# Joining the products of V of an attention head, and planning the order of a kernel's work in ten stretches

## The chip, the core and the metric

The kernel runs on one core of one Trainium2 chip. The metric is the time of the whole program on the device, in microseconds (us), as the median of several runs. Engines carry two names here: TensorE is PE in the profile (PEld are its weight loads), VectorE is DVE, ScalarE is ACT, GpSimd is POOL, and SyncE, which issues the transfers, is SP.

## What is computed

The reference is a backbone of two layers over 512 latent tokens and 256 context tokens of width 1024, in float32. Layer 0 attends to a neighbourhood on a grid with a position bias, layer 1 to a sliding window with grouped keys, sink logits and rotary embedding; latent queries see their local keys and all context keys in one softmax.

```
for i in range(2):
    u = modulate(rms_norm(h, g_mix[i]), shift1, scale1)
    q, k, v = projections of u, normed per head        # 16 heads of 64
    p = softmax(q k^T / 8 (+ bias or mask or sink), over local and context keys)
    h = h + gate1 * ((p v) @ wo)
    h = h + gate2 * (relu(modulate(rms_norm(h, g_mlp[i]), shift2, scale2) @ w1) ** 2 @ w2)
```

Shifts, scales and gates come from `ada_w`, a matrix of 1024 x 6144 for each layer. In layer 0 the context tokens are also queries, over the context alone.

## The kernel before

**Products.** Weights and activations are each split in a high and a low part (type fp32r), and a product is the sum of three on TensorE with 128 columns of the array (`mm`, `scores`, `proj1`). Products of V and the probabilities are done otherwise. V of a head has 64 columns, so `mm_halves` (line 722) issues two products for two different blocks of keys, one on columns 0 to 63 and one on columns 64 to 127 of the array; both halves add up in one PSUM bank, and `merge` (line 1103) adds the upper half to the lower with one copy and one addition. These products are in plain float32, which TensorE does in two passes. Two passes of two products make four records in the trace, shown as `128*64`. The modulation of layer 0 (`ada_pe`, line 787) uses 32 columns at a time (`128*32`).

**A head of layer 0** (`attn0`, line 1111; two heads to each of eight pairs `p`): scores of four blocks of queries and of the context; exponentials; probabilities scaled; then blocks of 128 x 128 transposed on TensorE into one of three PSUM banks (2, 3, 6), each bank copied to one of five slots of SBUF (`PTr`, `evac_pt`), and four calls of `mm_halves`: context keys, two of local keys, then the context's own queries. Latent and context sums take turns in bank 7.

**A head of layer 1** (`Head1`, line 1777): the same in `front` (scores, mask, exponentials) and `back` (transpositions, copies to three slots of `PTr`, line 1621, and three calls of `mm_halves` into bank 7). The front of a head is woven with the back of the one before, and the projections of the next four heads (`q1`) go between. Where the last heads run, the output projection (`wo1`) begins. Residuals `h` wait in DRAM during layer 1 and come back through four slots of SBUF (`h_slots`, line 1868).

**The order of the work** is not that of the code. All calls are recorded as steps of a plan with the steps that they depend on (`Plan.add`), each with a cost on its engine (`cost`, line 218). On TensorE a change between kinds of product has a cost of its own (`TURN`, line 291: "R" for 128 columns, "t" for transpositions, 64 and 32). `forward` (line 326) plays the plan once: each engine takes the ready step of lowest rank, and some steps choose between engines. `hurry` moves steps forward on whose account TensorE stood idle, `shaken` changes ranks at random, and `search` (line 464) keeps the best of many plays. It does so in two stretches: up to a step in the middle of the MLP of layer 0, judged by the start of that step, and from there to the end. Then every step is issued at one line (542), which the framework keeps in program order on each engine, with waits where data or buffers demand them. So every row of the trace names line 542, and rows are told apart by engine, operation and shapes.

Of the kernel before, what the change touches and what calls it, by code (L numbers as in the profile page):

```python
# [118 lines left out]
class Plan:  # L119
# [98 lines left out]
    def cost(self, x):  # L218
        if x.eng == "PE":
            kinds = []  # L220
            for f, args, kw in x.calls:
                out, a, b = args[:3]
                if f == "transpose":
                    kinds.append(("t", 128, 0, 128))
                else:
                    st, mv = a, b
                    kinds.append(("r" if st.dtype == R32 else "f", width(st)[0], geometry(out)[1], width(mv)[0]))
            kind, cols, _, n = kinds[0]
            if kind == "t":
                x.mode, x.occ, x.dur = "t", 109.0, 272.0  # L230
            elif kind == "r":
                x.occ, x.dur = ((n + 32) / 2.4 if n > 128 else 90.0), 389 - (512 - n) / 2.4
            elif cols == 128:
                x.occ = 2 * (n / 1.2 + 6)
                x.dur = x.occ + 150
            else:
                x.mode = cols
                at, runs = 999, []
                for _, _, p0, m in kinds:
                    if p0 <= at:  # L240
                        runs.append(0)
                    at = p0
                    runs[-1] = max(runs[-1], m)
                x.occ = sum(2 * (m / 1.2 + (47 if cols == 64 else 3)) for m in runs)
                x.dur = x.occ + 150
        elif x.eng == "SP":
            out, src = x.writes[0], x.reads[0]
            n, run = width(out)[0] * geometry(out)[2], 4 * min(geometry(y)[4][-1][1] for y in (out, src))
            if self.space(out) == "DRAM":
                n = math.prod(c for _, c in out.ap)  # L250
            x.bytes = 4 * n / (360.0 if run >= 2048 else 330.0 if run >= 1024 else 200.0 if run >= 512 else 100.0)
            x.occ = 620.0 if self.space(out) == "DRAM" else 430.0
        else:
# [210 lines left out]
    def search(self, rounds, tries, cut):  # L464
# [7 lines left out]
        rnd = random.Random(1)  # L472

        def of(rank, first, upto):
            s = self.forward(rank, first.copy(), upto)
            s.rank, s.last = rank, s.start[cut] if upto else max(s.end)
            return s

        def rounds_of(rank, first, upto, n, least=200):
            best = None  # L480
            for k in range(n):
                s = of(rank, first, upto)
                if not best or s.last < best.last:
                    best = s
                rank = self.hurry(rank if s.last < best.last * 1.004 else best.rank, s, least)
            return best

        first, rank = self.begin(), [float(x.i) for x in self.steps]
        for upto in (cut, None):
            found = [rounds_of(rank, first, upto, 3 * rounds)]  # L490
            for k in range(tries):
                found.sort(key=lambda s: s.last)
                found.append(rounds_of(self.shaken(found[k % 2].rank, rnd), first, upto, rounds, rnd.choice((100, 200))))
            first = best = min(found, key=lambda s: s.last)
        s = best
        for i, e in enumerate(s.eng):
            x = self.steps[i]
            if x.forms:
                x.eng = self.ALL[e]
                x.calls = [x.forms[x.eng]]  # L500
        self.plan = s
        place = {i: (k, e) for e, l in enumerate(s.order) for k, i in enumerate(l)}
        return [self.steps[i] for i in sorted(place, key=lambda i: (s.start[i], place[i][1], place[i][0]))]
# [16 lines left out]
def build(nc, tc, a):  # L520

    with ExitStack() as es:
        plan, regions, cut = _build(nc, tc, a, es)
        tiles, now, open_ = {}, -1, ExitStack()

        def real(x):
# [9 lines left out]
        for step in plan.search(ROUNDS, TRIES, cut):  # L536
# [9 lines left out]
ROUNDS, TRIES = 10, 24  # L546

LAST = 3

# [6 lines left out]
def _build(nc, tc, a, es):  # L556
    plan = Plan()
# [69 lines left out]
    regions = []  # L627
# [18 lines left out]
    Slots = Banks  # L646
# [72 lines left out]
    def mm(ps, st, mv, start, stop):  # L719
        pe.matmul(ps, st, mv, start=start, stop=stop)  # L720

    def mm_halves(pairs, start=False, stop=False):

        with together():
            for at, (out, st, mv) in zip((0, 64), pairs):
                pe.matmul(out[at : at + 64], st, mv, start=start, stop=stop, tile_position=(0, at))

    def split(H_, L_, x, eng=None):

# [202 lines left out]
    def bias_tables():  # L932

        for c in range(16):
            o = 128 - 8 * c
            load(bias_i[:, c * 8 : c * 8 + 8], a["rpb_i"][:, :, o : o + 256])
            load(bias_e[:, c * 8 : c * 8 + 8], a["rpb"][:, :, (7 - c % 8 + c // 8 * 8) * 8 :][:, :, 0:128])
            yield


    raw, raw0 = Ring(FA, FX, 768, 2), Ring(FA, FX, 1024, 2)
# [169 lines left out]
    def attn0(p, i):  # L1111
# [55 lines left out]
        for c in range(2):  # L1167
# [2 lines left out]
            for j, P in enumerate((A_, B_, C_)):  # L1170
                tr(ps, 64 + j * 128, P, c * 128)
            blocks.append((po, Vs(4 + c), evac_pt(ps, 0, 512)))
        mm_halves(blocks, start=True)
        yield
        ps = p_pt.next()
        tr(ps, 0, W_, 256)
# [1 line left out]
        tr(ps, 256, A_, 384)  # L1178
        tr(ps, 384, B_, 256)
        pt = evac_pt(ps, 64, 512)  # L1180
        mm_halves([(po[:, 0:192], Vs(0), pt[:, 0:192]), (po[:, 64:320], Vs(1), pt[:, 192:448])])
        yield
        ps = p_pt.next()
        tr(ps, 0, B_, 384)
# [1 line left out]
        tr(ps, 256, C_, 384)  # L1186
        tr(ps, 384, W_, 384)
        pt = evac_pt(ps, 0, 448)
        mm_halves([(po[:, 192:448], Vs(2), pt[:, 0:256]), (po[:, 320:512], Vs(3), pt[:, 256:448])], stop=True)
        merge(OT_lat[:, p], po, i)  # L1190
# [208 lines left out]
    for p in range(7):  # L1399
# [5 lines left out]
        else:  # L1405
            run(ad)
            p_mm = Banks(4, 5)
            weave(at, (qkv0(p + 1), 7))
    wo0.take(0, Stream(Ring(FA, FX, 1024, 2), [(a["wo0"][0, q], u) for q, u in enumerate((wx, wslots[2], wslots[0], wslots[3]))], 4))
    for p in range(7):  # L1410
        split_o(p, eng=v if p in (0, 2, 4) else g)
# [5 lines left out]
    split_o(7)  # L1417


    cut = []  # L1420

    def mlp(layer, T_ctx, stream, tmp, side, st_lat, st_ctx, between=None, after_ctx=None):
        if T_ctx:
# [119 lines left out]
        for c in range(NCH):  # L1543
            now = nxt
            if c == NCH // 2 and T_ctx:
                cut.append(next(x.i for x in reversed(plan.steps) if x.eng == "PE"))
            if c + 1 < NCH:
                nxt = mlp1(c + 1)
                if T_ctx or c:
# [45 lines left out]
        modulate(lambda f: hT_ctx[:, f], R_ctx, amod[layer][:, i, :, 1], mods[layer][:, 3 * i, :, 1], lambda f: uH_ctx[:, f], lambda f: uL_ctx[:, f], lambda f: ring.next(256))  # L1595

    wo0.rest(stream, Banks(0,1,7,2,3), *st, lambda: mod_lat(0, 1, tmp2))

    def between():
        st[1].finish()  # L1600
# [23 lines left out]

# [152 lines left out]
    class Head1:  # L1777
# [8 lines left out]
        def front(self):  # L1786
# [3 lines left out]
            for t in (1, 0, 2, 3):  # L1790
# [2 lines left out]
                inner = t in (1, 2)  # L1793
                if t == 0:
                    scores(ps, T1, T2, q0, with_context(K, 0))
                    mk = mask[:, 0:768].rearrange("p (s n) -> p s n", s=2)[:, :, 0:256]
# [23 lines left out]
        def back(self):  # L1820
# [32 lines left out]
            blocks.append(ctx(1))  # L1853
            yield
            ee = ends()
            mm_halves(blocks, start=True)
# [15 lines left out]
        sy.dma_start(h1[f], h_d[:, f])  # L1872

    kv1()
    heads = [Head1(h) for h in range(16)]
    for gr in range(4):
        seq = []
        n = 0
# [15 lines left out]
        if gr < 3:  # L1894
            load1(gr + 1)
            weave((go(), 24 if gr else 21), (q1(gr + 1), 8))
        else:
            wo1 = Wo(1, False, lambda ctx, f: hT_lat[:, f])
            wo1.take(0, Stream(raw, [(a["wo1"][0, q], u) for q, u in enumerate(wq + [wslots[6]])], 4, g))
# [20 lines left out]
    return plan, regions, cut[0]  # L1920

# [66 lines left out]
```

## Time and profile before

| what | before |
|---|---|
| median of 3 runs | 1621.09 us (1620.41 to 1621.33) |
| profiled execution | 1619.86 us, its span 1617.7 us |
| mean granted clock of TensorE | 0.999 |
| busy: TensorE, its weight loads | 1596.9 us (99%), 1332.1 us (82%) |
| busy: VectorE, ScalarE, GpSimd | 1174.1 us (73%), 814.0 us (50%), 248.3 us (15%) |
| transfers | 165.59 MB, 102 GB/s in the mean |

The span goes from the first to the last instruction of the profiled execution; its own time lies around it. Busy time counts records, which overlap on TensorE: the start of a product comes before the end of the one before it. So the time that TensorE spends on something is read from start to start. Layer 0's attention lies at about 60 to 425 us, layer 1's at about 1060 to 1225 us, MLPs and projections in between and behind.

### The profile page before, as it was taken

The page shows a single profiled execution, that of the slowest core. Times are in us where ns is not written, and L with a number is a line of the kernel's source. Part 1 is how long each engine was busy: PE and PEld are TensorE (multiplying, and loading weights), DVE is VectorE, ACT ScalarE, POOL GpSimd, SP SyncE. Part 2 cuts the span into 40 slices and gives each one's busy share as a digit, 9 for nine tenths or more (in the row PEclk, how much of TensorE's full clock was granted, in tenths as well). Part 3 has the DMA queues.
Part 4 walks back from the last instruction along what each step waited for, and adds up shares of the span by engine and source line. Part 5 has one row for each costly group of instructions (what it writes and reads, how often), then busy time and mean ns, then how long its engine had stood idle before and what let it go on. Part 6 is the DMA issues. An engine that isn't in the chain of part 4 may idle for free.

```text
span 1617.7 us, 24693 instructions
## 1 busy us (share of the span) xinstructions
PE 1596.9 (99%) x9356; PEld 1332.1 (82%) x9356; DVE 1174.1 (73%) x2376; ACT 814.0 (50%) x1627; POOL 248.3 (15%) x220
## 2 busy tenths in 40 slices
PE   8999999999999999999999999999999999999999
PEld 4788888887888888888888888787768888888887
DVE  4798777887488676676786767999996855556554
ACT  4687667776355242434442523677894533222220
POOL 0111111111123020312230211342200000000000
PEclk9999999999999999999999999999999999999999
DMA  9643343123324232333341422010024332222301
GB/s 347 198 134 98 116 128 99 49 65 118 102 78 147 91 129 92 119 117 129 120 141 54 142 92 78 24 43 27 20 73 163 105 105 91 102 94 79 104 27 52
DMA packets 57400, 165.59 MB, mean 102 GB/s; under 512 B 6593, under 2 KB 16193, under 8 KB 57153
## 3 DMA queue, kind: packets, MB, share of 16 engines
q1 hardware_dynamic: 57280, 164.01, 31.0%
q8 instruction: 73, 1.20, 0.3%
q14 instruction: 47, 0.38, 0.1%
HBM read 159.79 MB, written 7.34 MB: 103 GB/s over the span
## 4 chain that ended last, share of the span: by engine, by line
PE 92%; DVE 5%; ACT 2%; issue 1%; DMA 1%; POOL 0%; SPq 0%; DVEq 0%; ACTq 0%; POOLq 0%
PE pq L542 92%; DVE FA L542 2%; DVE RA L542 2%; DVE smalls L542 1%; ACT FA L542 1%; ACT RA L542 0%; ACT R L542 0%; DMA FA<-in_wqkv_dram 0%; DMA FA<-in_xT_dram 0%; POOL FA L542 0%; ACT smalls L542 0%; DVE R L542 0%; SPq L542 0%; DVEq L542 0%; DVE amod L542 0%
## 5 line engine op out<-in xcount | busy, mean ns | idle before, releaser
L542 PE MATMUL pq<-RA 128*128 128x512 f32 (+3 forms) x6560 | 1274.6, 348 | 6.9 <-ACT RA L542 2.8
L542 PEld LDWEIGHTS pq<-RA 128*128 128x128 f32 x6560 | 1053.5, 189 | 166.5 <-issue 14.5
L542 ACT CAST RA<-FA 128x1024 fp32r<-128x1024 f32 (+3 forms) x283 | 225.9, 812 | 347.6 <-PE pq L542 260.8
L542 DVE SCALAR_TENSOR_TENSOR FA<-pq,mods,FA 128x512 f32<-128x512 f32 (+1 forms) x413 | 263.5, 661 | 132.9 <-PE pq L542 131.6
L542 DVE TENSOR_TENSOR RA<-FA,RA 128x1024 fp32r<-128x1024 f32 (+3 forms) x248 | 244.4, 997 | 98.1 <-ACT RA L542 96.7
L542 PE MATMUL pq<-RA,R 128*128 128x512 f32 (+1 forms) x870 | 182.3, 352 | 0.0
L542 PEld LDWEIGHTS pq<-RA,R 128*128 128x128 f32 x870 | 143.7, 188 | 25.4 <-issue 0.8
L542 ACT ACTIVATE FA<-FA,smalls 128x512 f32<-128x512 f32 (+1 forms) x166 | 121.4, 741 | 26.8 <-DVE smalls L542 26.2
L542 POOL TENSOR_TENSOR RA<-FA,RA 128x512 fp32r<-128x512 f32 (+1 forms) x35 | 51.0, 1457 | 539.8 <-ACT RA L542 539.2
L542 PE MATMUL pq<-ident,FA 128*128 128x128 f32 x800 | 129.8, 276 | 3.2 <-DVE FA L542 1.9
L542 PEld LDWEIGHTS pq<-ident,FA 128*128 128x128 f32 x800 | 94.8, 140 | 26.4 <-issue 6.9
L542 DVE TENSOR_TENSOR R<-R,FA 128x1024 f32<-128x1024 f32 x84 | 103.8, 1260 | 15.0 <-ACT FA L542 7.8
L542 POOL TENSOR_SCALAR FA<-FA,s 128x1024 f32<-128x1024 f32 x24 | 78.4, 3265 | 221.7 <-DMA FA<-in_ada_w_dram 179.0
L542 POOL TENSOR_TENSOR FA<-FA,smalls 128x256 f32<-128x256 f32 (+2 forms) x81 | 59.8, 743 | 341.4 <-DVE smalls L542 249.3
L542 ACT ACTIVATE FA<-FA,s 128x1024 f32<-128x1024 f32 x60 | 68.9, 1151 | 69.5 <-POOL FA L542 54.0
L542 ACT ACTIVATE FA<-pq 128x512 f32<-128x512 f32 (+1 forms) x96 | 49.9, 522 | 82.6 <-PE pq L542 82.6
L542 DVE SCALAR_TENSOR_TENSOR FA<-pq,FA 128x512 f32<-128x512 f32 (+1 forms) x96 | 57.0, 596 | 45.4 <-ACT FA L542 45.2
L542 ACT ACTIVATE FA<-FA 128x256 f32<-128x256 f32 (+1 forms) x130 | 58.9, 455 | 47.7 <-DVE FA L542 42.7
L542 ACT COPY R<-pq 128x512 f32<-128x512 f32 (+4 forms) x145 | 68.6, 491 | 28.2 <-PE pq L542 25.7
L542 PE MATMUL pq<-R 128*64 128x512 f32 (+2 forms) x448 | 79.2, 463 | 0.7 <-DVE FA L542 0.7
L542 POOL TENSOR_TENSOR FA<-FA 128x256 f32<-128x256 f32 (+2 forms) x59 | 47.4, 816 | 191.5 <-ACT FA L542 130.5
L542 ACT COPY FA<-pq 128x256 f32<-128x256 f32 (+4 forms) x98 | 42.4, 433 | 57.1 <-PE pq L542 54.2
(84 smaller groups left out, 994.7 us busy)
## 6 DMA issues: line engine op xcount, KB each, us to landing
FA<-in_w_dram SPq DMA_DIRECT2D x128, 512.0 KB, 3.5
FA<-in_ada_w_dram SPq DMA_DIRECT2D x80, 512.0 KB, 3.8
FA<-in_wqkv_dram SPq DMA_DIRECT2D x24, 384.0 KB, 3.3
FA<-in_wo_dram SPq DMA_DIRECT2D x16, 512.0 KB, 3.4
FA<-in_ada_dram SPq DMA_DIRECT2D x10, 512.0 KB, 10.3
FA<-in_wq_dram SPq DMA_DIRECT2D x8, 512.0 KB, 3.5
R<-in_ada_dram SPq DMA_DIRECT2D x6, 512.0 KB, 10.9
FA<-in_xT_dram SPq DMA_DIRECT2D x4, 512.0 KB, 6.7
```

What stands on the lines that cost most here:

```text
L542: tc.keep_in_program_order(getattr(e, f)(*map(real, args), **{k: real(x) for k, x in kw.items()}))
```

## The change

**Products.** `mm_halves` takes lists of pairs, one list for each sum, and issues all of them in one step. `attn0` gathers its four calls in one at the end, `back` its three. The sum of the context's queries goes to one of the transposition banks rather than to bank 7. Layer 1 has five slots for copies rather than three; two of them hold 384 columns, one lies in the region `RX` and one behind the mask, which shrinks from 896 columns to 640, and the rope table moves by 128 columns. The cost of a step with several pairs is lowered by 38 ns for each further pair.

**Search.** `mark()` notes the last step of TensorE so far, and ten such marks are set: after pairs 0, 2, 4 and 6 of layer 0, after the output projection, in the middle of the MLP, after the keys of layer 1, and after three of its four groups of heads. For each stretch the search plays on to the end of the next one, keeps the best rank, and fixes the order up to the mark. Rounds go from 10 to 8 and tries from 24 to 16, for each stretch.

```diff
-                x.occ = sum(2 * (m / 1.2 + (47 if cols == 64 else 3)) for m in runs)
+                x.occ = sum(2 * (m / 1.2 + (47 if cols == 64 else 3)) for m in runs) - (38 * (len(runs) - 1) if cols == 64 else 0)
...
-            s.rank, s.last = rank, s.start[cut] if upto else max(s.end)
+            s.rank, s.last = rank, (max(s.free[pe], s.start[upto]) if upto else max(s.end)) - s.done
...
-        first, rank = self.begin(), [float(x.i) for x in self.steps]
-        for upto in (cut, None):
-            found = [rounds_of(rank, first, upto, 3 * rounds)]
+        source = [float(x.i) for x in self.steps]
+        first, rank, marks = self.begin(), source, cuts + [None]
+        for q, mark in enumerate(marks):
+            far = marks[min(q + 1, len(marks) - 1)]
+            found = [rounds_of(r, first, far, 2 * rounds) for r in ((rank, source) if q else (source,))]
...
-            first = best = min(found, key=lambda s: s.last)
+            best = min(found, key=lambda s: s.last)
+            rank = best.rank
+            if mark:
+                first = of(rank, first, mark)
...
-    def mm_halves(pairs, start=False, stop=False):
+    def mm_halves(*sums):
 
         with together():
-            for at, (out, st, mv) in zip((0, 64), pairs):
-                pe.matmul(out[at : at + 64], st, mv, start=start, stop=stop, tile_position=(0, at))
+            for pairs in sums:
+                for n, pair in enumerate(pairs):
+                    for at, (out, st, mv) in zip((0, 64), pair):
+                        pe.matmul(out[at : at + 64], st, mv, start=n == 0, stop=n == len(pairs) - 1, tile_position=(0, at))
...
-        po = p_pv.next()[:, 0:256]
-        mm_halves([(po, Vs(4 + c), pt[:, c * 256 : c * 256 + 256]) for c in range(2)], start=True, stop=True)
-        merge(OT_ctx[:, p], po, i)
+        pc = p_pt.next()[:, 0:256]
+
+        mm_halves(pairs, [[(pc, Vs(4 + c), pt[:, c * 256 : c * 256 + 256]) for c in range(2)]])
+        merge(OT_lat[:, p], po, i)
+        merge(OT_ctx[:, p], pc, i)
...
-    mask = FA[:, 4096:4992]
-    rope = FA[:, 4992:6016].rearrange("p (e t d) -> p e t d", e=4, t=4)
+    mask = FA[:, 4096:4736]
+    rope = FA[:, 5120:6144].rearrange("p (e t d) -> p e t d", e=4, t=4)
...
-    PTr = Slots(*(RX[:, 2176 + 512 * i : 2688 + 512 * i] for i in range(3)))
+    PTr = Slots(*(RX[:, 2176 + 512 * i : 2688 + 512 * i] for i in range(3)), RX[:, 3712:4096], FA[:, 4736:5120])
...
-            mm_halves(blocks, start=True)
             yield
-            blocks = [mid(1)]
-            mm_halves(ee)
+            mids = [mid(1)]
             yield
-            blocks.append(mid(2))
-            yield
-            mm_halves(blocks, stop=True)
+            mids.append(mid(2))
+            mm_halves([blocks, ee, mids])
```

How the order moves on TensorE in the attention of layer 0, a head of one of the later pairs, before. `pq7` is the PSUM bank of the sums of V, `pq2`, `pq3` and `pq6` the banks of the transpositions, `R00` the region with copied probabilities and V, `RA` the split operands; `x2` counts equal instructions in a row.

```order
L542 MATMUL pq7_72<-R00_124 64x512 x2
L542 MATMUL pq7_72<-R00_124 64x192
L542 MATMUL pq7_72<-R00_124 64x256 x2
L542 MATMUL pq7_72<-R00_124 64x192
L542 MATMUL pq4_69<-RA_63 128x512 x2
L542 MATMUL pq5_70<-RA_63 128x512
L542 MATMUL pq6_71<-ident_73,FA_64 128x128 x3
L542 MATMUL pq7_72<-R00_124 64x256 x2
L542 MATMUL pq1_66<-RA_63 128x512 x2
```

And a head of the change:

```order
L547 MATMUL pq5_70<-RA_63 128x384 x24
L547 MATMUL pq7_72<-R00_124 64x512 x2
L547 MATMUL pq7_72<-R00_124 64x192
L547 MATMUL pq7_72<-R00_124 64x256 x2
L547 MATMUL pq7_72<-R00_124 64x192
L547 MATMUL pq2_67<-R00_124 64x256 x2
L547 MATMUL pq6_71<-ident_73,FA_64 128x128 x3
```

The last pair, the context's own queries, has moved up to the others, into bank 2.

TensorE in the attention of layer 1, second head, before (`R20` is that layer's region with copied probabilities and V):

```order
L542 MATMUL pq4_69<-RA_63 128x256 x4
L542 MATMUL pq7_72<-R20_8853 64x512 x2
L542 MATMUL pq7_72<-R20_8853 64x256 x2
L542 MATMUL pq3_68<-ident_73,FA_64 128x128 x3
L542 MATMUL pq6_71<-ident_73,FA_64 128x128 x3
L542 MATMUL pq7_72<-R20_8853 64x384 x2
L542 MATMUL pq6_71<-ident_73,FA_64 128x128
```

And in the change:

```order
L547 MATMUL pq4_69<-RA_63 128x256 x3
L547 MATMUL pq7_72<-R20_8851 64x512 x2
L547 MATMUL pq7_72<-R20_8851 64x256 x2
L547 MATMUL pq7_72<-R20_8851 64x384
L547 MATMUL pq7_72<-FA_64,R20_8851 64x384
L547 MATMUL pq6_71<-ident_73,FA_64 128x128 x4
L547 MATMUL pq3_68<-ident_73,FA_64 128x128 x4
```

The two pairs of 384 columns now follow the others at once; the transpositions that fed them stand in front of all, and one of the two reads its copy from the slot behind the mask (`FA`).

SP's queue at the end of layer 1, before (`h_d` holds the residuals in DRAM, `in_w` are the weights of the MLP, `in_wo` of the output projection):

```order
L542 DMA FA<-in_w_dram 128x1024 x2
L542 DMA FA<-h_d 128x512
L542 DMA FA<-in_wo_dram 128x1024
L542 DMA FA<-in_w_dram 128x1024 x3
L542 DMA FA<-h_d 128x512 x3
```

And in the change:

```order
L547 DMA FA<-in_wo_dram 128x1024
L547 DMA FA<-in_w_dram 128x1024 x2
L547 DMA FA<-h_d 128x512
L547 DMA FA<-in_w_dram 128x1024 x2
L547 DMA FA<-h_d 128x512 x3
```

The fourth load of the residuals has moved behind the last load of the output projection's weights, with two loads of the MLP's behind it.

## Rows read from the trace of the kernel before

**Rows 1.** The page: busy time by engine, and the chain that ended last.

```profile
PE 1596.9 (99%) x9356; PEld 1332.1 (82%) x9356; DVE 1174.1 (73%) x2376; ACT 814.0 (50%) x1627; POOL 248.3 (15%) x220
...
PE 92%; DVE 5%; ACT 2%; issue 1%; DMA 1%; POOL 0%; SPq 0%; DVEq 0%; ACTq 0%; POOLq 0%
```

**Rows 2.** Waits of PE, 0 to 60 us: total us, times, longest.

```profile
PE pq L542 <- DVE R L542: 5.9, 1, 5.9
PE pq L542 <- ACT RA L542: 1.8, 1, 1.8
```

**Rows 3.** Windows: us, busy by engine, PEclk, DMA share, GB/s.

```profile
0.00:60.00 60.00, 52.20 (x412) 35.16 (x413) 35.09 (x87) 27.62 (x58) 4.65 (x14) 0.97 0.80 284
```

**Rows 4.** Waits of PE, 60 to 1618 us: three of six groups.

```profile
PE pq L542 <- DVE FA L542: 2.9, 5, 1.1
...
PE pq L542 <- ACT R L542: 0.8, 2, 0.5
PE pq L542 <- DVE smalls L542: 0.5, 2, 0.3
```

**Rows 5.** The page's groups: busy us, mean ns | idle before.

```profile
L542 PE MATMUL pq<-R 128*64 128x512 f32 (+2 forms) x448 | 79.2, 463 | 0.7 <-DVE FA L542 0.7
```

**Rows 6.** Timeline of PE, layer 1: start us, length us, operation, records.

```profile
1105.01 1.51 PE L542 MATMUL pq<-R 128*64 128x512 f32 x8
1106.45 0.51 PE L542 MATMUL pq<-RA 128*128 128x512 f32 x1
...
1180.92 1.08 PE L542 MATMUL pq<-R 128*64 128x512 f32 x4
1181.93 0.96 PE L542 MATMUL pq<-RA 128*128 128x512 f32 x3
```

**Rows 7.** Timeline of PE, end of layer 0's attention and the output projection.

```profile
407.35 0.65 PE L542 MATMUL pq<-R 128*64 128x256 f32 x4
407.93 1.81 PE L542 MATMUL pq<-RA 128*128 128x256 f32 x13
409.67 1.84 PE L542 MATMUL pq<-R 128*64 128x512 f32 x12
...
446.51 2.43 PE L542 MATMUL pq<-RA 128*128 128x256 f32 x19
448.78 0.86 PE L542 MATMUL pq<-RA,R 128*128 128x256 f32 x6
```

**Rows 8.** Timeline of PE, layer 1, a run between transpositions.

```profile
1085.98 0.49 PE L542 MATMUL pq<-ident,FA 128*128 128x128 f32 x3
1086.40 0.87 PE L542 MATMUL pq<-R 128*64 128x384 f32 x4
1087.19 0.33 PE L542 MATMUL pq<-ident,FA 128*128 128x128 f32 x1
1087.36 0.27 PE L542 MATMUL pq<-ident,R 128*128 128x128 f32 x1
```

**Rows 9.** Timeline of PE and its weight loads, the last head's first run.

```profile
1220.00 1.51 PE L542 MATMUL pq<-R 128*64 128x512 f32 x8
1220.49 0.14 PEld L542 LDWEIGHTS pq<-R 128*64 128x64 f32 x2 [0.29 <-issue]
```

**Rows 10.** Groups by shape, 1060 to 1235 us: busy us, mean ns | idle before.

```profile
L542 ACT COPY R<-pq 128x512 f32<-128x512 f32 x39 | 21.5, 588 | 1.1 <-PE pq L542 0.7
L542 DVE TENSOR_TENSOR FA<-pq,FA 64x512 f32<-64x512 f32 x16 | 11.0, 686 | 5.3 <-ACT FA L542 5.0
```

**Rows 11.** Timeline of all engines, behind the last head.

```profile
1223.65 16.61 PE L542 MATMUL pq<-RA 128*128 128x512 f32 x80
1228.97 2.30 DVE L542 SCALAR_TENSOR_TENSOR FA<-pq,mods,FA 128x512 f32<-128x512 f32 x2
```

**Rows 12.** Transfers: issues, KB each, median us from issue to landing.

```profile
FA<-h_d SPq DMA_DIRECT2D x8, 256.0 KB, 3.3
```

**Rows 13.** Windows in the attention of layer 0 and of layer 1 (columns as above).

```profile
100.00:350.00 250.00, 250.00 (x1690) 216.51 (x1689) 196.68 (x605) 175.95 (x480) 33.64 (x48) 1.00 0.31 95
1060.00:1210.00 150.00, 148.35 (x976) 110.88 (x977) 142.34 (x419) 131.84 (x304) 33.12 (x41) 1.00 0.13 43
```

More of the change, by code (lines that the diff above doesn't have):

```diff
@@ L462, in shaken, with search @@
         return [r + shift.setdefault(i // size, rnd.gauss(0.0, span)) for i, r in enumerate(rank)]
-    def search(self, rounds, tries, cut):
+    def search(self, rounds, tries, cuts):
         self.epochs()
@@ L471, in search @@
                 self.steps[j].succ.append(x.i)
-        rnd = random.Random(1)
+        rnd, pe = random.Random(1), self.ALL.index("PE")
         def of(rank, first, upto):
             s = self.forward(rank, first.copy(), upto)
-            s.rank, s.last = rank, s.start[cut] if upto else max(s.end)
+            s.rank, s.last = rank, (max(s.free[pe], s.start[upto]) if upto else max(s.end)) - s.done
             return s
@@ L484, in rounds_of @@
                     best = s
-                rank = self.hurry(rank if s.last < best.last * 1.004 else best.rank, s, least)
+                rank = self.hurry(rank if s.last < best.last + 4000 else best.rank, s, least)
             return best
-        first, rank = self.begin(), [float(x.i) for x in self.steps]
-        for upto in (cut, None):
-            found = [rounds_of(rank, first, upto, 3 * rounds)]
+        source = [float(x.i) for x in self.steps]
[3 more added lines that the diff above has]
+            found = [rounds_of(r, first, far, 2 * rounds) for r in ((rank, source) if q else (source,))]
             for k in range(tries):
                 found.sort(key=lambda s: s.last)
-                found.append(rounds_of(self.shaken(found[k % 2].rank, rnd), first, upto, rounds, rnd.choice((100, 200))))
-            first = best = min(found, key=lambda s: s.last)
+                found.append(rounds_of(self.shaken(found[k % 2].rank, rnd), first, far, rounds, rnd.choice((100, 200))))
+            best = min(found, key=lambda s: s.last)
+            rank = best.rank
+            if mark:
+                first = of(rank, first, mark)
         s = best
@@ L522, in build @@
     with ExitStack() as es:
-        plan, regions, cut = _build(nc, tc, a, es)
+        plan, regions, cuts = _build(nc, tc, a, es)
         tiles, now, open_ = {}, -1, ExitStack()
@@ L534, in turn @@
                 tiles[k, j] = pool.tile([128, n], dtype, name=f"R{k}{j}", tag="R")
-        for step in plan.search(ROUNDS, TRIES, cut):
+        for step in plan.search(ROUNDS, TRIES, cuts):
             while step.epoch is not None and now < step.epoch:
@@ L543, in build @@
         open_.close()
-ROUNDS, TRIES = 10, 24
+ROUNDS, TRIES = 8, 16
 LAST = 3
@@ L938, in bias_tables, with mark @@
             yield
+    cuts = []
+    def mark():
+        cuts.append(next(x.i for x in reversed(plan.steps) if x.eng == "PE"))
     raw, raw0 = Ring(FA, FX, 768, 2), Ring(FA, FX, 1024, 2)
@@ L1172, in attn0 @@
             blocks.append((po, Vs(4 + c), evac_pt(ps, 0, 512)))
-        mm_halves(blocks, start=True)
+        pairs = [blocks]
         yield
@@ L1180, in attn0 @@
         pt = evac_pt(ps, 64, 512)
-        mm_halves([(po[:, 0:192], Vs(0), pt[:, 0:192]), (po[:, 64:320], Vs(1), pt[:, 192:448])])
+        pairs.append([(po[:, 0:192], Vs(0), pt[:, 0:192]), (po[:, 64:320], Vs(1), pt[:, 192:448])])
         yield
@@ L1188, in attn0 @@
         pt = evac_pt(ps, 0, 448)
-        mm_halves([(po[:, 192:448], Vs(2), pt[:, 0:256]), (po[:, 320:512], Vs(3), pt[:, 256:448])], stop=True)
-        merge(OT_lat[:, p], po, i)
+        pairs.append([(po[:, 192:448], Vs(2), pt[:, 0:256]), (po[:, 320:512], Vs(3), pt[:, 256:448])])
         yield
@@ L1408, in _build @@
             weave(at, (qkv0(p + 1), 7))
+        if p in (0, 2, 4, 6):
+            mark()
     wo0.take(0, Stream(Ring(FA, FX, 1024, 2), [(a["wo0"][0, q], u) for q, u in enumerate((wx, wslots[2], wslots[0], wslots[3]))], 4))
@@ L1417, in _build @@
     split_o(7)
-    cut = []
     def mlp(layer, T_ctx, stream, tmp, side, st_lat, st_ctx, between=None, after_ctx=None):
@@ L1545, in mlp @@
             if c == NCH // 2 and T_ctx:
-                cut.append(next(x.i for x in reversed(plan.steps) if x.eng == "PE"))
+                mark()
             if c + 1 < NCH:
@@ L1597, in _build @@
     wo0.rest(stream, Banks(0,1,7,2,3), *st, lambda: mod_lat(0, 1, tmp2))
+    mark()
     def between():
@@ L1795, in front @@
                     scores(ps, T1, T2, q0, with_context(K, 0))
-                    mk = mask[:, 0:768].rearrange("p (s n) -> p s n", s=2)[:, :, 0:256]
+                    mk = FA[:, 4096:4864].rearrange("p (s n) -> p s n", s=2)[:, :, 0:256]
                     col[t] = {0: 256, 1: 384, 4: 0, 5: 128}
@@ L1855, in back @@
             ee = ends()
-            mm_halves(blocks, start=True)
             yield
-            blocks = [mid(1)]
-            mm_halves(ee)
+            mids = [mid(1)]
             yield
-            blocks.append(mid(2))
-            yield
-            mm_halves(blocks, stop=True)
+            mids.append(mid(2))
+            mm_halves([blocks, ee, mids])
             merge(OT_lat[:, h // 2], po, h % 2)
@@ L1874, in _build @@
     kv1()
+    mark()
     heads = [Head1(h) for h in range(16)]
@@ L1896, in _build @@
             weave((go(), 24 if gr else 21), (q1(gr + 1), 8))
+            mark()
         else:
@@ L1919, in _build @@
     mlp(1, False, stream, Ring(FA, FX + 5120, 512, 5), iter(()), None, None, between=lambda: half_done(256))
-    return plan, regions, cut[0]
+    return plan, regions, cuts
 def layout(inputs):
```

## The prediction

> **What bounds the kernel now.** I read the page's first parts, then the waits of TensorE, then its timeline around the products of V, and last the busy time of all engines by stretch. The first part and the chain [rows 1] say that TensorE is busy 99% of the span, and that the chain which ends last runs on it for 92%: whatever shortens TensorE's own stream shortens the kernel, as long as nothing else takes its place. The waits of TensorE say how little idle time there is: 5.9 + 1.8 = 7.7 us in the first 60 us [rows 2], where the inputs arrive (the 16 DMA engines are busy 80% there [rows 3]), and 8.8 us in all the rest, in six groups from 2.9 down to 0.5 us [rows 4]. So the gain can't come mainly from waits. It has to come from what TensorE does between its products.
>
> The products of V are the only ones that use 64 of the array's columns (448 records [rows 5], two passes for each of 224 instructions). I call a stretch in which they follow each other without another product between them a run. Three readings show what a run costs beside its columns.
>
> Inside a run: four records of 512 columns alone last from 1180.92 to the next product at 1181.93, 1.01 us; the same four with four of 256 behind them last from 1105.01 to 1106.45, 1.44 us [rows 6]. So four records of 256 cost 0.43 us where they are joined to a run. Alone they last from 407.35 to 407.93, 0.58 us [rows 7]. A run that goes saves 0.15 us.
>
> At its ends, beside ordinary products: 19 products of 256 columns in one stretch last 2.27 us, 0.1195 us each (446.51 to 448.78); 13 of them between two runs last 1.74 us (407.93 to 409.67) where 13 x 0.1195 makes 1.55 [rows 7]. Leaving one run and entering the next costs 0.19 us, 0.095 an end.
>
> At its ends, beside transpositions: three of them before a run last 0.42 us (1085.98 to 1086.40), where a transposition has 0.11; so an entry costs 0.09. After that run the first lasts 0.17 and not 0.11, an exit costs 0.06 [rows 8].
>
> **The change, part by part.**
>
> *Joined products.* In the order of the kernel before I count 69 runs (34 in layer 0, 35 in layer 1), in the order of the change 32: one for each head of a layer. So the change does what it says, and 37 runs go. Inside them: 37 x 0.15 = 5.6 us. Of their 74 ends, 43 lie at ordinary products (22 entries, 21 exits): 43 x 0.095 = 4.1 us. 27 lie at transpositions: 11 entries x 0.09 + 16 exits x 0.06 = 2.0 us. Four lie at the 32-column products of the modulation, which had a turn of their own: nothing. On the other side, runs of V and of those 32-column products touched each other on eight entries and now on four, and two more 32-column runs appear; I take the 0.19 us of two ends for each joint lost, 4 x 0.19 = 0.8 us. Sum: 5.6 + 4.1 + 2.0 - 0.8 = **10.9 us less**, 6.1 of it in layer 1 and 4.8 in layer 0. All of it lies on TensorE, hence on the path.
>
> The trace shows that a run's weights are loaded while its products go on: two loads at 1220.49, inside the products that start at 1220.00 and last 1.51 us [rows 9]. If the loads were not hidden between the pairs that are now joined, each of the 37 joints would wait for two of them, 37 x 0.14 = 5.2 us; this is a rival below. The Trainium skill, "TensorE: Matmul & The Clock Gate", Part 3 (packing small matmuls), says that a weight load overlaps products in flight only when their row groups differ, and all of these products use the same 128 rows; by that rule the 5.2 us are lost and the sum comes to 1614.
>
> *Copies are held longer.* A head copies five tiles of transposed probabilities out of PSUM, and all five are now held until its products have run. Layer 0 keeps its five slots; layer 1 gets five in place of three, two of them 384 wide and cut from the mask. Five tiles in five slots means that the next head's first copy waits for this head's products. In the order of the change, 10 or more other products stand between the last transposition and the run in 17 of the 32 heads, at most one in six (before: in 19 of the 69 runs); and the 16 heads of layer 1 fill some 150 us, over 9 us each, so I cost this at nothing; the cover is that other work. If it is gone, the price is the copy (0.59 us) and the merge that empties the accumulator (0.69 us) [rows 10]; that is the slower rival below.
>
> *Context accumulator.* The context sum of a head goes to one of the three transposition banks rather than to bank 7 again. It frees bank 7 for a head's whole period, and takes one bank from the transpositions for as long as two merge operations last. I cost it at nothing, with the same cover.
>
> *Mask, rope, and the reload of h.* The first slot for reloading h now overlaps the new tile slot, so its load waits for the last head's products. In the trace the last run ends at 1223.65, where the output projection goes on, and the first sum that reads h starts at 1228.97 [rows 11]; a load of h lands 3.3 us after its issue [rows 12]. 1223.65 + 3.3 = 1226.95 leaves 2.0 us. Behind that load SP's queue holds weight loads for the next stage only. Nothing.
>
> *The search.* It moves instructions on every engine: it is what decides the 8.8 us of waits. Nothing in the trace of before prices a different order; the bounds are the 8.8 us that could go, and as much again that could appear. The model of costs that the search goes by is the old one but for the price of joints, and it has sought these waits before, only over longer stretches; so I take a third of them, 3 us less.
>
> *What layer 1 can take.* In 1060 to 1210 us VectorE is busy for 142.3 of 150 us and ScalarE for 131.8, against 148.4 for TensorE; in layer 0 (100 to 350 us) VectorE has 196.7 of 250 [rows 13]. Taking 6.1 us from TensorE in a stage where VectorE has 7.7 us of room in all will not pass fully, since VectorE also has to wait for scores, and between its first and last operation on the heads of that layer it has 424 instructions in the new order and 426 in the old. I take 2 us back, between 0 and the whole 6.1.
>
> Sum: -10.9 - 3 + 2 = -11.9 us. The profiled execution took 1619.86 us (span 1617.7), 1.2 us under the median of 1621.09; its sum would give 1608.0, and against the median **1609 us**.
>
> **The rivals.**
>
> *The search removes the waits too.* Then 10.9 + 8.8 us go: 1601.4. For it: each stretch is now tried over and over with the one behind it in view. Against: waits in layer 1 come from VectorE, which has no room.
>
> *The loads of joined pairs show.* 5.2 us of the gain go, 1614. For it: a run standing alone does pay for its first loads. Against: with loads between all pairs, 0.43 us for four joined records of 256 against 0.58 alone could not be.
>
> *VectorE becomes the bound of layer 1.* Then only layer 0 gives its 4.8 us: 1616.3. For it: the row of 1060 to 1210 [rows 13]. Against: VectorE's busy time includes pieces that it can give to the idle POOL (33 of 150 us). The Trainium skill, "TensorEngine Tiling (Array Packing)", PSUM Bottleneck, says that the copies out of PSUM may become the bound once TensorE is faster; its advice, to share them between ScalarE and VectorE, this kernel already follows.
>
> *The five slots chain the heads (slower).* Place: the first copy of each head of layer 1, which can start only when the products of the head before are done. If TensorE runs out of other work there, every head pays a copy and a merge, 0.59 + 0.69 = 1.28 us; 16 x 1.28 = 20.5 us, less the 10.9: 1631. It decides the sign from 10.9 / 16 = 0.7 us per head. Against it: TensorE's waits for a copy (ACT R) are one of the smaller groups in [rows 4], 0.8 us in all, and that with three slots.
>
> *The order gets worse elsewhere.* Ten short stretches, each fixed for good, against two long ones: 11 us of new waits would eat the gain, about 1621, no change.
>
> **How the numbers follow.** Chances: forecast 0.55 (its own range 1604 to 1614), waits removed too 0.17, loads 0.03, VectorE 0.14, slots 0.05, worse order 0.06. The range 1600.5 to 1618 leaves out the slots, the worse order and the lower half of the second case, 0.05 + 0.06 + 0.08. A measurement of this kernel can tell about 0.2% (3.2 us) from no change. Faster by more: all of forecast, waits and loads, and most of VectorE's case, 0.87; within it: the rest of that case and most of the worse order, 0.07; slower: slots and the rest, 0.06.
>
> **What would show it.** Right: 32 runs of 64-column products in the timeline, one per head, each entered and left at the prices above; TensorE's busy time down by about 11 us with the same 9356 products; waits of TensorE after 60 us at 5 to 8 us. Layer 1's part is right if VectorE's busy share rises there to about 97% and the stage shortens by some 4 us. Wrong: waits on ACT R at the transpositions or on copies' slots in every head (slots); a stage 1060 to 1210 that keeps its length (VectorE); waits after 60 us above 15 us (order).

## The result, and the profile after

| what | before | after |
|---|---|---|
| median | 1620.75 us (1619.78 to 1621.33, 4 runs) | 1606.82 us (1605.22 to 1607.7, 4 runs) |
| ratio, 95% interval | | 0.9915, 0.9899 to 0.993 |
| profiled execution, its span | 1619.86 us, 1617.7 us | 1607.38 us, 1605.6 us |
| runs of 64-column products | 69 | 32 |

The change takes 13.9 us, 0.85%. The forecast was 1609.0 us, in a range of 1600.5 to 1618. The page of the changed kernel, busy time by engine and the chain that ended last, which answer to [rows 1]:

```profile
PE 1586.9 (99%) x9356; PEld 1336.9 (83%) x9356; DVE 1178.4 (73%) x2385; ACT 810.7 (50%) x1624; POOL 237.1 (15%) x214
...
PE 92%; DVE 4%; DMA 2%; ACT 1%; SPq 1%; issue 1%; POOL 0%; DVEq 0%; ACTq 0%
```

TensorE issues the same 9356 products and is busy 10.0 us less (1596.9 before). It still carries 92% of the chain: the kernel has the same bound as before, with a shorter stream.

The waits of TensorE from 60 us to the end, beside [rows 4] (total us, times, longest):

```profile
PE pq L547 <- DVE RA L547: 1.5, 2, 1.2
PE pq L547 <- DVE smalls L547: 1.0, 1, 1.0
PE pq L547 <- ACT R L547: 0.9, 2, 0.7
PE pq L547 <- DVE FA L547: 0.9, 1, 0.9
PE pq L547 <- ACT RA L547: 0.9, 3, 0.5
PE pq L547 <- ACT FA L547: 0.3, 1, 0.3
PE pq L547 <- DVE R L547: 0.2, 1, 0.2
PE pq L547 <- POOL FA L547: 0.2, 1, 0.2
```

They sum to 5.9 us, 2.9 less than the 8.8 of before. The row for the slots is `ACT R`, a wait for a copy of probabilities: 0.9 us, and 0.8 before.

The windows of the two attentions, beside [rows 13] (us; busy PE, PEld, DVE, ACT, POOL with instructions; PEclk, DMA share, GB/s):

```profile
100.00:350.00 250.00, 249.64 (x1710) 219.83 (x1707) 203.09 (x625) 180.10 (x493) 37.78 (x51) 1.00 0.29 95
1060.00:1210.00 150.00, 148.50 (x998) 114.13 (x997) 144.67 (x418) 135.10 (x309) 28.20 (x37) 1.00 0.14 49
```

In these 150 us TensorE passes 998 products where it passed 976 (the same times, not quite the same work), and VectorE is busy for 144.67 of 150 us, 96.4%, where it was 142.34.

Two heads in TensorE's timeline (start us, length us, operation, records), one of layer 0 and one of layer 1:

```profile
361.67 2.25 PE L547 MATMUL pq<-RA 128*128 128x384 f32 x12
363.85 2.27 PE L547 MATMUL pq<-R 128*64 128x512 f32 x16
366.05 0.55 PE L547 MATMUL pq<-ident,FA 128*128 128x128 f32 x3
...
1085.71 1.83 PE L547 MATMUL pq<-R 128*64 128x512 f32 x9
1087.05 0.49 PE L547 MATMUL pq<-FA,R 128*64 128x384 f32 x1
1087.37 0.49 PE L547 MATMUL pq<-R 128*64 128x384 f32 x1
1087.38 0.49 PE L547 MATMUL pq<-FA,R 128*64 128x384 f32 x1
1087.79 1.09 PE L547 MATMUL pq<-ident,FA 128*128 128x128 f32 x8
```

All pairs of a head are one run. Layer 1's twelve records last from 1085.71 to 1087.79, 2.08 us. The rows of before make it 1.44 us for the four of 512 and four of 256 [rows 6], plus 0.80 for the four of 384 standing alone [rows 8] (1086.40 to 1087.19, 0.79 in these digits), less the 0.15 that a joint saves: 2.09. So the joint costs nothing beside its columns.

**Where the time went.** I took every product's start from the trace and added up the time from it to the next product's start, by kind. The last product starts at 1613.7 us of the span before and at 1601.2 after, 12.5 less. The runs took 75.4 us and take 68.6: 6.8 less (forecast: 5.6). But a wait behind a run is counted with it, and before there is one, of 0.8 us:

```profile
376.63 0.65 PE L542 MATMUL pq<-R 128*64 128x256 f32 x4 [0.66 <-DVE FA L542]
378.06 1.73 PE L542 MATMUL pq<-RA 128*128 128x512 f32 x8 [0.78 <-DVE RA L542]
```

Without it the runs take 6.0 us less. Their ends are counted in the traces and priced as in the prediction for each kind of neighbour, not measured one by one: they came to 16.1 us and come to 10.5, 5.5 less before rounding (forecast: 4.1 + 2.0 - 0.8 = 5.3). The prices hold in the trace of before: in the median an entry costs 0.09 us behind 128-column products and 0.09 behind transpositions, an exit 0.11 and 0.06. The modulation's products and those of the statistics take 0.5 more. What is left, all that the other products last beyond their own columns, waits included, goes from 33.6 to 32.9: 0.7 less, or 1.5 with the wait of 0.8.

### The profile page after: what moved, and what is told of

Same layout as the page of the kernel before. It is cut to its first block, busy times and chain, and to the rows that moved or that the text cites. A ratio compares the mean times of both kernels' runs of the same rounds, so it can differ in the third digit from the quotient of the medians.

```text
span 1605.6 us, 24687 instructions
## 1 busy us (share of the span) xinstructions
PE 1586.9 (99%) x9356; PEld 1336.9 (83%) x9356; DVE 1178.4 (73%) x2385; ACT 810.7 (50%) x1624; POOL 237.1 (15%) x214
## 4 chain that ended last, share of the span: by engine, by line
PE 92%; DVE 4%; DMA 2%; ACT 1%; SPq 1%; issue 1%; POOL 0%; DVEq 0%; ACTq 0%
PE pq L547 92%; DVE FA L547 2%; DVE RA L547 2%; SPq L547 1%; DMA FA<-in_ada_w_dram 1%; ACT FA L547 1%; DVE smalls L547 0%; ACT RA L547 0%; DMA FA<-in_wqkv_dram 0%; DMA FA<-in_xT_dram 0%; DMA FA<-in_cT_dram 0%; DVE R L547 0%; DMA bias_i<-in_rpb_i_dram 0%; ACT R L547 0%; ACT smalls L547 0%
## 5 line engine op out<-in xcount | busy, mean ns | idle before, releaser
L547 DVE TENSOR_TENSOR RA<-FA,RA 128x1024 fp32r<-128x1024 f32 (+3 forms) x251 | 248.6, 1001 | 98.1 <-ACT RA L547 95.4
L547 PE MATMUL pq<-ident,FA 128*128 128x128 f32 x800 | 125.0, 275 | 2.8 <-DVE FA L547 0.9
L547 POOL TENSOR_TENSOR RA<-FA,RA 128x512 fp32r<-128x512 f32 (+1 forms) x32 | 45.3, 1417 | 508.8 <-ACT RA L547 489.8
L547 POOL TENSOR_TENSOR FA<-FA,smalls 128x256 f32<-128x256 f32 (+2 forms) x79 | 63.6, 809 | 336.9 <-DVE smalls L547 253.8
L547 POOL TENSOR_SCALAR FA<-FA,s 128x1024 f32<-128x1024 f32 x24 | 75.1, 3129 | 198.4 <-DMA FA<-in_ada_w_dram 158.0
L547 ACT COPY FA<-pq 128x256 f32<-128x256 f32 (+5 forms) x111 | 47.6, 428 | 74.1 <-PE pq L547 59.9
L547 POOL TENSOR_TENSOR FA<-FA 128x256 f32<-128x256 f32 (+2 forms) x58 | 44.1, 773 | 230.4 <-ACT FA L547 190.3
L547 ACT COPY R<-pq 128x512 f32<-128x512 f32 (+4 forms) x130 | 62.4, 503 | 22.7 <-PE pq L547 20.6
L547 PE MATMUL pq<-R 128*64 128x256 f32 (+3 forms) x416 | 70.7, 452 | 0.0
## 6 DMA issues: line engine op xcount, KB each, us to landing
FA<-in_ada_dram SPq DMA_DIRECT2D x10, 512.0 KB, 10.3
```

## The experiments

My theory: the joined products give the turns (about 11 us), and the new search a few microseconds of waits. One rival gives all to the search; another says that joined steps make waits of their own, which the search takes out again, so that neither part alone is worth its term. A comparison of single kernels carries the luck of an order, so I also tried other random starts.

**The change without its search.** Products as in the change, and the function `search` of before with its two stretches, rounds and tries.

```diff
-        for step in plan.search(ROUNDS, TRIES, cuts):
+        for step in plan.search(ROUNDS, TRIES, cuts[5]):
...
-ROUNDS, TRIES = 8, 16
+ROUNDS, TRIES = 10, 24
```

> The products joined as in the change (32 runs), planned by the search of the kernel before (two stretches, 30 and 10 rounds, 24 tries). If the gain is the turns that went, 37 runs fewer at 0.3 us each give about 11 us: 1608 to 1611 us. If the new search is what gains, this stays at 1616 to 1621 us. If long stretches find worse places for joined products, it lies above 1612 us with waits of TensorE after 60 us above 10 us.

**The search without the join.** `attn0`, `back`, slots, mask and rope as before, under the search in ten stretches. (Its ten marks make eleven, the last from the tenth mark to the end; I keep the short name.)

```diff
-        pairs = [blocks]
+        mm_apart(blocks, start=True)
...
-            mm_halves([blocks, ee, mids])
...
+            mm_apart(blocks, stop=True)
```

> The products apart as before (three or four steps a head, old slots), planned by the new search in ten stretches. Its order has 65 runs of V's products, 4 fewer than before. If the gain is the turns, 4 x 0.3 = 1.2 us and about 1 us of waits go: 1617 to 1621 us. If the search is what gains, 1607 to 1612 us.

Measured: the join with the old search 1614.13 us, ratio 0.9966 (0.9954 to 0.9978); the new search with separate products 1620.78 us, 0.9998 (0.9989 to 1.0007). Alone the join gives 6.4 us and the search nothing; together they give 13.9. The waits of TensorE after 60 us under the old search, the joined products (five of seven groups):

```profile
PE pq L542 <- POOL FA L542: 3.1, 2, 1.7
PE pq L542 <- DVE smalls L542: 1.7, 4, 1.0
PE pq L542 <- ACT R L542: 1.6, 3, 0.7
PE pq L542 <- DVE FA L542: 1.6, 2, 1.0
PE pq L542 <- ACT RA L542: 1.6, 2, 1.2
```

With the two groups left out (0.7 and 0.6) they are 10.9 us, against 5.9 in the change. By the same sum of starts, the turns went nearly in full (6.0 us inside the runs when waits behind them are taken out, 5.2 at their ends), but the remainder grew by about 5 us. So the old search pays nearly half of the gain back. The list of waits shows 2.1 us of that (10.9 against 8.8 before); the rest stands in no row. Nor do these waits lie at the joined products: in the two attentions (60 to 425 and 1010 to 1225 us) they are 6.3 us, against 7.8 before. What is new lies in the stages behind the attentions, 4.5 us where before had 0.8 and the change has none (the first row from 425 to 1010 us, the others from 1225 us on):

```profile
PE pq L542 <- POOL FA L542: 1.7, 1, 1.7
...
PE pq L542 <- POOL FA L542: 1.4, 1, 1.4
PE pq L542 <- ACT RA L542: 1.2, 1, 1.2
```

The new search alone, on separate products, leaves waits of 10.0 us after 60 us; its two largest groups:

```profile
PE pq L547 <- DVE FA L547: 3.5, 6, 1.3
PE pq L547 <- POOL FA L547: 3.1, 2, 2.3
```

**The old search with another start.** As the first, with another seed.

```diff
-        rnd = random.Random(1)
+        rnd = random.Random(2)
```

> The joined products under the old search, as in the run with the old search, but with another random start (2 instead of 1). If the 7.3 us between that run (1614.13 us) and the change (1606.82 us) are what the old search leaves in joined steps, this kernel lies within about 2 us of 1614 (the seeds of the new search lay within 1.2 us of each other), at 1612 to 1616, and its waits of TensorE after 60 us are again about 10 us. If it was an unlucky order, it lies near the change: 1609 us or less, with waits after 60 us of 6 to 7 us.

1618.23 us, 0.9982 (0.9973 to 0.9991). So the first seed was not an unlucky one: waits after 60 us are 11.7 us here. They lie elsewhere, though: 9.1 us in the two attentions and 2.5 behind them. The median lies 2 us above the range that I gave, and the granted clock goes with it: the mean was 0.995 to 0.997 in nine of eleven runs, and the two runs at 0.998 and 0.999 took 1614.45 and 1614.26. More of that below.

**Other starts for the change.** Its own search with seeds 2 and 3.

```diff
-        rnd, pe = random.Random(1), self.ALL.index("PE")
+        rnd, pe = random.Random(2), self.ALL.index("PE")
```

> The change with another seed of the random numbers of its search, nothing else. It says how far a plan's luck goes: if turns decide, within 2 us of the change, 1605 to 1609 us; if the change's gain was partly a lucky order, up to 1613 us.

> The change with a third seed. As for the second: 1605 to 1609 us if turns decide, up to 1613 us if the order of the change was a lucky one.

1607.98 us (0.9921, 0.9906 to 0.9936) and 1607.15 us (0.9916, 0.9902 to 0.9929). Three starts of the new search lie within 1.2 us; two of the old one at 1614.13 and 1618.23. With joined products the new search is thus worth 6 us at the least in the starts tried (1614.13 - 1607.98). The kernel of before and the new search on separate products were run with one start each. The new search also makes more plays, with 16 tries in each of eleven stretches against 24 in each of two; the old search with as many was not run.

**The same order, each run cut in two.** The plan of the change, played as it is; only at the issue the last pair of each joined step is held back until TensorE's next step has been issued. That makes 64 runs of the 32.

```diff
+            halves = step.eng == "PE" and step.mode == 64
...
+            issue(step, step.calls[:-2] if halves else step.calls)
+            if halves:
+                held = [step, step.calls[-2:]]
+            elif held and step.eng == "PE":
+                issue(*held)
```

> The plan and order of the change, but the last pair of each head's joined step is issued behind the next step of TensorE, so that 64 runs stand where the change has 32; nothing else is moved. If turns cost what the trace of before shows, 32 more runs at 0.15 us inside and 0.15 to 0.19 us at their ends add 10 us: 1615 to 1619 us. If the gain came from the new places of steps (the search) and not from the turns, it stays within 2 us of the change, 1605 to 1609 us.

1616.04 us, 0.9975 (0.9966 to 0.9985): 9.2 us for 32 cuts. The timeline of the same head:

```profile
360.93 4.41 PE L546 MATMUL pq<-RA 128*128 128x384 f32 x24
365.27 1.84 PE L546 MATMUL pq<-R 128*64 128x512 f32 x12
367.04 0.33 PE L546 MATMUL pq<-ident,FA 128*128 128x128 f32 x1
367.30 0.65 PE L546 MATMUL pq<-R 128*64 128x256 f32 x4
367.88 0.44 PE L546 MATMUL pq<-ident,FA 128*128 128x128 f32 x2
```

Twelve records last 1.77 us (365.27 to 367.04) and the four that were cut off 0.58 (367.30 to 367.88), together 2.35 where the joined run lasts 2.20 (363.85 to 366.05): 0.15 us for the cut inside. The transposition between them lasts 0.26 where it has 0.11 among its like: 0.15 for an exit and an entry. Over the kernel the runs take 7.1 us more, but five waits that lie behind cut runs are counted with them, 1.9 us in all; the longest:

```profile
1100.17 0.33 PE L546 MATMUL pq<-ident,FA 128*128 128x128 f32 x1 [0.63 <-DVE FA L546]
```

So the cuts add 5.2 us inside the runs, 0.16 each, and 5.1 at their ends by the same prices: 10.3 in all, of which 8.7 show in the span. The waits after 60 us are 6.6 us, against 5.9 in the change, so shorter waits are not what makes up the difference of 1.6; it stays open. That is the turns by themselves, with no search between the two kernels.

**One layer joined at a time**, under the new search: layer 0 alone (only `back`, slots, mask and rope as before), and layer 1 alone (only `attn0` as before). Layer 0 alone:

```diff
+            mm_apart(blocks, start=True)
...
-            mm_halves([blocks, ee, mids])
...
+            mm_apart(blocks, stop=True)
```

> New search, products joined in layer 0 alone; layer 1 has its steps and three slots as before. 48 runs (16 and 32). If turns decide, it lies 17 x 0.3 = 5 us under the kernel with the new search and products apart, at 1612 to 1616 us. If VectorE bounds layer 1, so that nothing is to be had there, it is as fast as the change, 1605 to 1609 us.

Layer 1 alone:

```diff
-        mm_halves(pairs, [[(pc, Vs(4 + c), pt[:, c * 256 : c * 256 + 256]) for c in range(2)]])
...
+        mm_apart([(po, Vs(4 + c), pt[:, c * 256 : c * 256 + 256]) for c in range(2)], start=True, stop=True)
```

> New search, products joined in layer 1 alone with its five slots; layer 0 as before. 48 runs (32 and 16). If turns decide there too, 17 runs fewer than with the new search and products apart give 5 us: 1612 to 1616 us. If VectorE or the five slots hold layer 1 back, 0 to 2 us: 1617 to 1621 us.

1610.66 us (0.994, 0.9928 to 0.9953) and 1616.08 us (0.9969, 0.996 to 0.9979). The stages are parted by a product that every order has at the same place in the work, the statistics ahead of layer 1. Its row without any join, under the new search:

```profile
1014.88 1.02 PE L547 MATMUL pq<-FA,ones 128*128 128x512 f32 x2
```

and with layer 0 joined:

```profile
1009.99 1.02 PE L547 MATMUL pq<-FA,ones 128*128 128x512 f32 x2
```

4.9 us earlier, and 6.6 at equal clock: the second has 3.4 us more at half clock near its start, some 1.7 us. The other pair (1017.01 with layer 1 alone joined, 1010.14 in the change) says 6.9, of which about 1.7 is such a stretch in the former's first stage. Layer 1's join is read behind that product, up to the last product's start: 595.2 us without and 591.1 with it where layer 0 is joined, 4.1 less; 600.1 and 596.1 where it is not, 4.0 less, or 5.7 without such a stretch in the second. The two kernels without layer 1's join differ by 4.9 us there (600.1 and 595.2): that much is luck of the order, or of what the first stage leaves behind, and it is as large as the term itself.

The whole times say more than the stages. Under the new search layer 0's join takes 10.1 us where layer 1 is separate (1620.78 to 1610.66) and 9.3 where it is joined (1616.08 to 1606.82); layer 1's takes 4.7 and 3.8. So the first kernel came out below its 1612 to 1616 us, and the second at their upper end. Where layer 0 is joined the waits after 60 us fall as well, from 10.0 to 4.8 us and from 9.6 to 5.9; in the first case 2.3 of that is one wait in the MLP, outside the edit, which lies in the 4.9 us above as well. With one start for each kernel, how much of this is the join and how much the order can't be told.

**How far ahead a stretch is judged.** At its own end; two marks ahead; more tries; both.

```diff
-            far = marks[min(q + 1, len(marks) - 1)]
+            far = mark
```

> The change with each stretch judged at its own end and not at the end of the next one. If looking on matters, orders that leave work undone behind the mark are kept and 2 to 8 us come back: 1609 to 1615 us. If it doesn't, within what seeds make, 1605 to 1609 us.

```diff
-ROUNDS, TRIES = 8, 16
+ROUNDS, TRIES = 10, 32
```

> The change with 10 rounds and 32 tries for each stretch in place of 8 and 16. If the waits that are left are orders not yet found, 1 to 3 us go, 1603 to 1606 us; if they are held by VectorE and the transfers, it stays at 1605 to 1609 us, where the seeds lie.

```diff
-            far = marks[min(q + 1, len(marks) - 1)]
+            far = marks[min(q + 2, len(marks) - 1)]
```

> The change with each stretch judged at the end of the second one behind it. Judged at its own end it took 1612.1 us, at the end of the next one 1606.8. If looking on goes on to pay, 1603 to 1605 us; if one stretch is far enough, 1605 to 1609 us; if more room to search with the same tries costs, 1609 us or more.

The last has this edit and the 10 and 32 above.

> Two stretches ahead and 10 rounds with 32 tries together. If either pays, at or under the better of the two, down to 1602 us; if the waits left are not a matter of search, 1605 to 1609 us.

| judged at | tries | median | ratio (95%) |
|---|---|---|---|
| own end | 16 | 1612.13 us | 0.9945 (0.9932 to 0.9959) |
| next end (the change) | 16 | 1606.82 us | 0.9915 (0.9899 to 0.993) |
| next end | 32 | 1608.03 us | 0.9924 (0.9912 to 0.9937) |
| two ahead | 16 | 1607.08 us | 0.9915 (0.9902 to 0.9929) |
| two ahead | 32 | 1605.61 us | 0.9912 (0.9899 to 0.9926) |

All but the change have one start each. Stretches judged at their own ends are 2 us under the first run of the old search, with intervals that touch; judging each at the next end is worth another 5.3 us, with intervals that do not meet. Farther ahead or more tries give nothing that can be told apart: the lowest median, two ahead with more tries, has an interval that covers the change's.

## Why the prediction was right, and where not

**The turns: right.** The forecast was 10.9 us. The trace gives 6.0 inside the runs and, at the forecast's own prices, 5.5 at their ends; the modulation and the statistics take 0.5 back: 11.0. Runs went from 69 to 32 as counted. The term inside a run holds: 6.0 / 37 is 0.16 us where I took 0.15 from one pair of rows, and the cut runs give 0.16 again. The order held still and its runs cut, 9.2 us come back for 32 cuts, against 10 expected; this is the run that shows the cause.

**By layer: right in size in the stages, not shown by the whole times.** Layer 0: forecast 4.8, measured 4.9 and 6.9, or 6.6 and 5.2 at equal clock. Layer 1: forecast 6.1 less 2 for VectorE, 4.1; measured 4.1 and 4.0 to 5.7. The luck of an order, 4.9 us in one comparison, is as large as either term, and the whole times give layer 0's join twice its forecast, with fewer waits beside the turns. Where layer 0 is joined already, joining layer 1 takes only about 4.5 us of turns away, for 16 runs, and the remainder gives about 1 back. So about 1 us and not 2 came back, and that VectorE is what takes it is not shown, though its share rose as forecast (96.4% against "about 97%").

**The search: its term failed, the sum held.** The step was "so I take a third of them, 3 us less". The waits did fall by 2.9 us, as forecast. But I had priced the search as a term of its own, and with separate products it gives nothing. With joined products, about 5 us of the turns do not reach the span under the old search, and the new one gets them back. I had given that no price: that the waits fell by just 3 us is luck, not the mechanism that I had named. What makes the 5 us is not shown. Copies held longer, which I costed at nothing, would show as waits for a copy: `ACT R` is 1.6 us in the first run of the old search, 0.5 in the second and 0.8 before, and in the first run the new waits lie outside the attentions. Why the new search doesn't also help separate products stays open too.

**The rivals.** *Loads of joined pairs show*: no; 2.08 us for a run of 2.09, where two loads that show at its joint would have made it 2.23. The rule behind that rival, in the Trainium skill, "TensorE: Matmul & The Clock Gate", Part 3 (a weight load overlaps products in flight only when the row groups differ), does not hold for these products, which share all their rows; the measurement decides. *VectorE bounds layer 1*: no; the layer's join gave about 4 us. The Trainium skill, "TensorEngine Tiling (Array Packing)", PSUM Bottleneck, warns that copies out of PSUM may become the bound; VectorE is busy for 96.4% of that stretch, and no run here shows it as the bound. *Five slots chain the heads*: no; `ACT R` 0.9 us in all, with the heads' runs joined. *The search removes the waits too*: a third of them. *Worse order elsewhere*: not in the change. The rival laid it to ten short stretches; with joined products it is the two long ones that cost 6 us and more, though short stretches judged at their own ends do give 5.3 us back.

## What to carry to other kernels

A switch between kinds of product has three prices on TensorE, on entering, on leaving and inside the run, and each can be read from start to start of neighbouring rows, once the waits between them are taken out; count the runs and multiply. When steps are merged, seek the order around them again: here the same edit was worth 2 to 6 us in the old way of ordering and 14 in the new one, and neither half alone tells it. Try a second random start before believing a difference of a few microseconds between two orders.

## What I had not expected

**TensorE runs at half clock for stretches that change with the order, and from run to run.** In the profile of before, the granted clock falls to half (1.2 GHz) once near the start, from 20.9 to 24.3 us; in the change it stays there from 21.2 to 28.0. The windows of before:

```profile
20.00:25.00 5.00, 4.84 (x42) 2.89 (x42) 1.83 (x4) 0.74 (x4) 0.00 (x0) 0.66 1.02 406
25.00:30.00 5.00, 5.00 (x24) 3.95 (x24) 3.27 (x7) 3.72 (x8) 1.29 (x2) 1.00 1.02 407
```

and of the change:

```profile
20.00:25.00 5.00, 4.72 (x40) 2.96 (x41) 1.82 (x4) 0.88 (x4) 0.00 (x0) 0.62 1.00 401
25.00:30.00 5.00, 5.00 (x18) 4.08 (x17) 2.69 (x6) 3.13 (x7) 0.99 (x1) 0.70 1.03 410
```

18 products instead of 24 pass in the second 5 us. 3.4 us more at half clock are some 1.7 us, by my estimate (half of that time's columns), that the change gives away there. The order alone doesn't fix this: in twenty runs of the kernel of before the mean granted clock lies between 0.997 and 1.0, and the times between 1623.26 and 1617.2 us. The joined products under the old search's second start show what such stretches cost. That kernel is at half clock for 17.1 us, in four stretches, at 19.2, 53.3, 377.6 and 1265.1 us. TensorE's timeline at the third, and behind it at the fourth (idle time and its releaser in brackets):

```profile
377.50 2.03 PE L542 MATMUL pq<-RA 128*128 128x256 f32 x6 [2.02 <-DVE RA L542]
...
1262.83 0.70 PE L542 MATMUL pq<-FA,ones 128*128 128x256 f32 x2 [1.34 <-POOL FA L542]
...
1265.61 0.58 PE L542 MATMUL pq<-RA,R 128*128 128x256 f32 x1 [1.25 <-ACT RA L542]
```

The clock fell behind a wait of 2.02 us in the one and in the second of two waits, of 1.34 and 1.25 us, in the other. Six products of 256 columns behind the first last 2.03 us; six that the change has near the same place last 1.20:

```profile
374.58 1.20 PE L547 MATMUL pq<-RA 128*128 128x256 f32 x6
```

So a wait that an order leaves can cost more than its own length. Its length alone doesn't say so: the new search on separate products has a wait of 2.3 us (its `POOL FA` row above), and its clock falls only once, near the start. Which orders meet it, and why some runs of one kernel and not others, is not settled here.

**A sum from start to start takes waits for turns.** The cut runs seem to add 12.2 us on TensorE, and 1.9 of these are waits that stand behind a run; before, 0.8 of the runs' 75.4 us were one. With the waits in, a run's inside came out at 0.18 us in one comparison and 0.22 in the other; without them it is 0.16 in both, beside the 0.15 of single rows.
